# Half-block products after Strassen in 5 of 11 pairs of weight tiles of the down projections of a two-layer decoder

## The chip, the core and the metric

The kernel runs on one core of one Trainium2 chip. A core has five engines that run beside each other and meet through semaphores: TensorE (PE: matrix products, results into PSUM, 8 banks of 128 x 512 float32), VectorE (DVE) and ScalarE (ACT) (elementwise work), GpSimd (POOL), and SyncE (SP), whose queue starts the transfers from HBM to the on-chip memory (SBUF). The metric is device time in microseconds (us); less is better. The time before is the median of three runs.

## What is computed

Sequence 512, width 1024, inner width of the feed-forward part 2816, all float32, two layers. Layer 0 mixes tokens by pooling, layer 1 by attention; both end in the same feed-forward part, whose second product is what the change is about:

```python
def conv_ffn(h, w_up, conv_w, conv_b, w_down):
    u = h @ w_up
    u = causal_dwconv(u, conv_w, conv_b)
    a, g = jnp.split(u, 2, axis=-1)
    return (jax.nn.silu(g) * a) @ w_down

def reference(x, ...):
    for i in range(DEPTH):
        ...
        x = x + conv_ffn(rmsnorm(x, norm_g[i, 1]), w_up[i], conv_w[i], conv_b[i], w_down[i])
    return rmsnorm(x, final_norm)
```

So `w_down` is 2816 x 1024 per layer, and the left operand (the gated activation) is 512 x 2816.

## The kernel before

**Numbers.** Matrix products run in a reduced float32 format. To keep float32 accuracy every operand is split into a high and a low half (`split`, lines 141 to 144: ACT copies `hi`, DVE subtracts to get `lo`), and each product is three matmuls (`mm3`, lines 159 to 163): high x high, high x low, low x high.

**Tiles.** The 512 tokens are 4 tiles of 128 (index t), the 2816 inner channels 22 tiles of 128 (index f or k), taken in 11 pairs (kk). The 1024 output columns are two halves of 512 (dh). The residual stream stays in SBUF as `xt[t]`.

**Up projection** (`ffn`, lines 385 to 397). For each f two products give the gate and the value channel; `gate` (lines 376 to 383) does the convolution (`conv`), SiLU and the product, and splits the result into `ah`, `al`, tiles of 128 channels x 512 tokens from `big` (tag T, 44 buffers). These are the stationary operands of the down projection.

**Down projection** (lines 399 to 424). Per column half four PSUM banks, one per token tile, collect all 22 k tiles. `chunk` (lines 151 to 157) loads two k tiles of weights, 128 x 1024 float32, 512 KB, into `raw` (3 buffers) and takes `hi` and `lo` (5 buffers each); `split` fills these; then 2 k x 4 t x 3 matmuls of 128 x 128 by 128 x 512 follow. In the second half the last three chunks are kept and multiplied token tile by token tile, so that each bank is added into `xt` (line 423) while PE goes on with the next. `after(t, dh)` goes on from there: in layer 0 (`to_n2`) the norm and the transposes for the attention, in layer 1 (`finish`) the final norm and the output.

**Order.** Only PE's order is that of the program text (`manual_schedule` for PE around everything but the start). The instructions of DVE, ACT, POOL and the transfers are put in order by a planner at build time, by priority in the order of the text and by when it reckons that their inputs and buffers are there; so work that is ready can run well ahead of its place in the text. On the chip each engine takes its own queue in order. Buffers with one tag rotate: `wide` (tag h, 4 buffers of 128 x 1024) serves norms and scratch, `scratch` (tag w, 6 buffers of 128 x 512) the convolutions, `Normed` takes the two buffers of tag H (128 x 4096 each) for the transposed, split input of the up projection, `bank` the eight PSUM banks.

Of the kernel before, what the change touches and what calls it, by code (L numbers as in the profile page):

```python
# [8 lines left out]
F32 = mybir.dt.float32  # L9
F32R = mybir.dt.float32r  # L10
AF = mybir.ActivationFunctionType
ALU = mybir.AluOpType
AX = mybir.AxisListType

P = 128
S = 512
D = 1024
NT = S // P
KD = D // P
DFF = 2816  # L20
NF = DFF // P
H = 8
# [12 lines left out]
VALUES, WEIGH, TURN = 2, 3, 5  # L35
RATES = 1.34, .6, 1.0
START = 1
AT = [(2, 1), (3, 0)]
CONSTS = P + S + 2 * 4 * P + 4 * 16

# [23 lines left out]
def trunk(ctx, tc, x, norm_g, pool_w, pool_scale, kv_norm, w_kv, wq, lam, subln_g, wo,  # L64
          w_up, conv_w, conv_b, w_down, final_norm, consts, out):
    nc = tc.nc
# [3 lines left out]
    hp = ctx.enter_context(tc.tile_pool(name="hp", bufs=1))  # L70
# [7 lines left out]
    def bank(name):  # L78
        return psum.tile([P, S], F32, tag="ps", name=name)

    def big(name, dt=F32R):
        return tp.tile([P, S], dt, tag="T", bufs=44, name=name)
# [4 lines left out]
    def scratch(name, dt=F32):  # L87
        return work.tile([P, S], dt, tag="w", bufs=6, name=name)

    def wide(name):  # L90
        return work.tile([P, D], F32, tag="h", bufs=4, name=name)

    def v3(t, a):
        return t.rearrange("p (a b) -> p a b", a=a)
# [6 lines left out]
    xt = [const.tile([P, D], F32, name=f"x{t}") for t in range(NT)]  # L101
# [35 lines left out]
    for i in (1, 2):  # L137
        n = S if i == 1 else 64
        nc.sync.dma_start(out=bands[i][:, :n], in_=consts[:, P + S * (i + 1):P + S * (i + 1) + n])

    def split(src, hi, lo):

        nc.scalar.copy(hi, src)  # L143
        nc.vector.tensor_tensor(lo, src, hi, ALU.subtract)  # L144
# [6 lines left out]
    def chunk(src, a, b, name):  # L151

        raw = wp.tile([P, a * b], F32, tag="raw", bufs=3, name=f"raw_{name}")
        hi = wp.tile([P, a * b], F32R, tag="hi", bufs=5, name=f"hi_{name}")
        lo = wp.tile([P, a * b], F32R, tag="lo", bufs=5, name=f"lo_{name}")
        nc.sync.dma_start(out=v3(raw, a), in_=src)
        return raw, hi, lo

    def mm3(ps, l, r, first, last):
        (lh, ll), (rh, rl) = l, r  # L160
        nc.tensor.matmul(ps, lh, rh, start=first, stop=False)  # L161
        nc.tensor.matmul(ps, lh, rl, start=False, stop=False)  # L162
        nc.tensor.matmul(ps, ll, rh, start=False, stop=last)  # L163

    def cols(pair, a, b):
        return tuple(v[:, a:b] for v in pair)
# [73 lines left out]
    def up_chunk(l, m):  # L240
        return chunk(w_up[l, :, m * P:(m + 1) * P].rearrange("(k p) c -> p k c", p=P), KD, P, f"u{l}_{m}")

    def up_weights(l, m):
        raw, hi, lo = up_chunk(l, m)
        split(raw, hi, lo)
        return hi, lo
# [5 lines left out]
    def product(l, m, ps, w, hT, a, b):  # L252
        for k in range(KD):
            mm3(ps[:, a:b], cols(w, k * P, (k + 1) * P), hT.k(k, a, b), k == 0, k == KD - 1)
# [16 lines left out]
    r0, h0, pin, d, pw, pout, pup = {}, {}, {}, {}, {}, {}, {}  # L271
# [76 lines left out]
    def vectors(_):  # L348
# [6 lines left out]
                 s=pool_split, o=pool_out, r=pool_add, q=n1.rms, v=n1.scale, t=n1.turn, u=n1.split,  # L355
                 H=up_high, L=up_low, p=up_product, c=vectors, W=warm)
# [6 lines left out]
    def ffn(l, hT, cw, ws, pss, after):  # L363


        act = []

        def conv(ps, m, name):
            y = scratch(f"cv_{name}")
            w = [v[:, m:m + 1] for v in cw]  # L370
            nc.scalar.activation(y, ps, AF.Identity, bias=w[3], scale=w[2])
            nc.vector.scalar_tensor_tensor(y[:, 1:], ps[:, :S - 1], w[1], y[:, 1:], ALU.mult, ALU.add)
            nc.vector.scalar_tensor_tensor(y[:, 2:], ps[:, :S - 2], w[0], y[:, 2:], ALU.mult, ALU.add)
            return y

        def gate(f, pg, pa):
            y = conv(pg, NF + f, f"{l}_{NF + f}")
            nc.scalar.activation(y, y, AF.Silu)
            a = conv(pa, f, f"{l}_{f}")
            nc.vector.tensor_tensor(a, a, y, ALU.mult)  # L380
            ah, al = big(f"ah{l}_{f}"), big(f"al{l}_{f}")
            split(a, ah, al)
            act.append((ah, al))

        for n, w in enumerate(ws):
            product(l, n, pss[n], w, hT, S // 2, S)
        for f in range(EARLY):
            gate(f, pss[2 * f], pss[2 * f + 1])
        for f in range(EARLY, NF):
            pss = []  # L390
            for half in (1, 0):
                m = half * NF + f
                w = up_weights(l, m)
                ps = bank(f"pu{l}_{m}")
                product(l, m, ps, w, hT, 0, S)
                pss.append(ps)
            gate(f, *pss)

        held = 3
        for dh in range(2):  # L400
            pss = [bank(f"pd{l}{dh}{t}") for t in range(NT)]

            def down(t, kk, w):
                for k2 in range(2):
                    k = 2 * kk + k2
                    mm3(pss[t], cols(act[k], t * P, (t + 1) * P), cols(w, k2 * S, (k2 + 1) * S),
                        k == 0, k == NF - 1)

            kept = []
            for kk in range(NF // 2):  # L410
                raw, hi, lo = chunk(w_down[l, kk * 2 * P:(kk + 1) * 2 * P, dh * S:(dh + 1) * S]
                                    .rearrange("(k p) c -> p k c", p=P), 2, S, f"d{l}_{dh}_{kk}")
                split(raw, hi, lo)
                if dh == 1 and kk >= NF // 2 - held:
                    kept.append((kk, (hi, lo)))
                    continue
                for t in range(NT):
                    down(t, kk, (hi, lo))
            for t in range(NT):
                for kk, w in kept:  # L420
                    down(t, kk, w)
                part = xt[t][:, dh * S:(dh + 1) * S]
                nc.vector.tensor_tensor(part, pss[t], part, ALU.add)
                after(t, dh)

    n2 = Normed("n2", None)

    def to_n2(t, dh):
# [3 lines left out]
        if t > 1:  # L432
            n2.tensors(t - 2)

    ffn(0, n1, cw0, [w[1:] for w in up0], pup, to_n2)


# [5 lines left out]
                      in_=lam.rearrange("l a b -> l (a b)").to_broadcast([P, 4 * HD]))  # L443
# [149 lines left out]
    def wo_add(ps, t, dh):  # L593
        part = xt[t][:, dh * S:(dh + 1) * S]
        nc.vector.tensor_tensor(part, ps, part, ALU.add)
# [67 lines left out]

    for i in range(START):
        next(filler)
# [19 lines left out]
    for t in range(2, NT):  # L685
        for dh in range(2):
            ps = bank(f"pw4{t}{dh}")
            for h in range(4, H):
                wo_part(ps, t, dh, h, h == 4, h == H - 1)
            wo_add(ps, t, dh)  # L690
            if (t, dh) in AT:
                n3.tensors(AT.index((t, dh)))
        n3.vectors(t)
# [27 lines left out]
    for n in range(2 * EARLY):  # L721
        raw, hi, lo = up_chunk(1, (n + 1) % 2 * NF + n // 2)
        split(raw, hi, lo)
        up1.append((hi, lo))
    for n in range(2 * EARLY):
        pup.append(bank(f"pu1_{n}"))
        product(1, n, pup[n], up1[n], n3, 0, S // 2)
        if n in (0, 1):
            n3.tensors(2 + n)
    ffn(1, n3, [columns(r) for r in conv_rows(1)], up1, pup, finish)  # L730


# [29 lines left out]
```

## Time and profile before

| | |
|---|---|
| median of 3 runs | 1008.89 us (1007.28 to 1009.53) |
| the profiled execution's own time | 1007.95 us |
| its span, first to last instruction | 1006.2 us |
| up projection of layer 0, most of it (65.0 to 279.6) | 214.6 us |
| down projection of layer 0 (279.6 to about 403) | about 123 us, the next norm's transposes among it |
| down projection of layer 1 (about 880 to 999) | about 119 us |
| HBM read / written | 92.44 MB / 2.10 MB |

The rest of the span is the pooling (to about 40 us) and the attention (about 403 to 650 us). How to read the lines that follow below: a row of the groups gives line, engine, operation, output and inputs, shapes and count, then total busy time and the mean of one in ns, then the idle time of that engine just before and what ended it. A row of the timeline begins with start and duration in us, and ends with the idle time before it and its releaser. A row of the stretches gives its bounds, its length, and each engine's busy time with the number of instructions, then PE's granted clock, the share of the DMA engines and GB/s. PE is the matmul, PEld the loading of the stationary operand beside it. A line number can be a helper's: line 144 is every low half, line 143 every high half, lines 161 to 163 every matmul of `mm3`; the name of the tile tells which (`pd` the down banks, `pu` the up banks, `d` in `raw_d`, `hi_d`, `lo_d` the down weights).

### The profile page before, as it was taken

Reading aid. Unit: us, or ns where it says so; the run is one execution under the profiler, and the core shown is the slowest. Engines: PE = TensorE matmul, PEld = TensorE weight load, DVE = VectorE, ACT = ScalarE, POOL = GpSimd, SP = SyncE. Lnnn points to the kernel's source line nnn. Section 1 sums busy time; section 2 is a strip of 40 time slices with the busy share of each in tenths; the row PEclk is TensorE's granted clock in tenths of the full one; section 3 lists DMA queues with packets and bytes.
Section 4 is the critical chain, followed back from the end, with each engine's and each line's share of the span. In section 5 each row is a group of like instructions: output and inputs, shape, how many; then the busy total and the mean of one; then the engine's idle time right before and its main releaser. Section 6 shows DMA issues by size and latency. Waiting matters only on the chain.

```text
span 1006.2 us, 12339 instructions
## 1 busy us (share of the span) xinstructions
PE 991.4 (99%) x4870; PEld 838.3 (83%) x4870; DVE 569.7 (57%) x872; ACT 426.9 (42%) x671; POOL 85.7 (9%) x113
## 2 busy tenths in 40 slices
PE   8999999999999999999999999999999999999997
PEld 8998888888888888778888887988888888888885
DVE  5766656656632323557766797576566566532213
ACT  5554443444432213446756662464444434422211
POOL 4500000000000001261220101000000000000001
PEclk9999999999999999999999999999999999999999
DMA  7333233233232321243213111243332332332312
GB/s 259 109 105 105 85 104 101 88 105 94 94 110 85 114 98 49 71 139 105 64 42 105 64 43 42 84 126 95 94 105 88 101 104 85 105 94 95 105 42 83
DMA packets 128707, 95.33 MB, mean 95 GB/s; under 512 B 3329, under 2 KB 111498, under 8 KB 128650
## 3 DMA queue, kind: packets, MB, share of 16 engines
q1 hardware_dynamic: 128650, 94.55, 30.4%
q8 instruction: 38, 0.62, 0.2%
q14 instruction: 19, 0.16, 0.0%
HBM read 92.44 MB, written 2.10 MB: 94 GB/s over the span
## 4 chain that ended last, share of the span: by engine, by line
PE 96%; DVE 1%; DMA 1%; ACT 0%; issue 0%; SPq 0%; POOL 0%; DVEq 0%; POOLq 0%; ACTq 0%
PE pu L161 16%; PE pu L162 16%; PE pu L163 16%; PE pd L163 8%; PE pd L161 8%; PE pd L162 8%; PE sc L531 2%; PE po L560 2%; PE pw L163 1%; PE pj_k L161 1%; PE pj_k L162 1%; PE pw L162 1%; PE pw L161 1%; PE pj_k L163 1%; PE pj_q L162 1%; PE pj_q L161 1%
## 5 line engine op out<-in xcount | busy, mean ns | idle before, releaser
L144 DVE TENSOR_TENSOR lo_u<-raw_u,hi_u 128x1024 fp32r<-128x1024 f32 x84 | 103.3, 1232 | 126.9 <-ACT hi_u L143 126.7
L161 PE MATMUL pu<-n3h,hi_u 128*128 128x512 f32 (+1 forms) x384 | 142.9, 372 | 0.0
L161 PE MATMUL pu<-n1h,hi_u 128*128 128x512 f32 (+1 forms) x384 | 142.8, 372 | 0.0
L162 PE MATMUL pu<-n3l,hi_u 128*128 128x512 f32 (+1 forms) x384 | 142.6, 371 | 0.0
L162 PE MATMUL pu<-n1l,hi_u 128*128 128x512 f32 (+1 forms) x384 | 142.6, 371 | 0.0
L163 PE MATMUL pu<-n1h,lo_u 128*128 128x512 f32 (+1 forms) x384 | 142.6, 371 | 0.0
L163 PE MATMUL pu<-n3h,lo_u 128*128 128x512 f32 (+1 forms) x384 | 142.6, 371 | 0.0
L144 DVE TENSOR_TENSOR lo_d<-raw_d,hi_d 128x1024 fp32r<-128x1024 f32 x44 | 53.9, 1226 | 147.1 <-ACT hi_d L143 147.1
L161 PE MATMUL pd<-hi_d,ah 128*128 128x512 f32 x352 | 137.0, 389 | 0.0
L163 PE MATMUL pd<-hi_d,al 128*128 128x512 f32 x352 | 136.9, 389 | 0.0
L162 PE MATMUL pd<-lo_d,ah 128*128 128x512 f32 x352 | 136.9, 389 | 0.0
L143 ACT CAST hi_u<-raw_u 128x1024 fp32r<-128x1024 f32 x84 | 88.1, 1051 | 64.2 <-PE pu L162 59.4
L143 ACT CAST hi_d<-raw_d 128x1024 fp32r<-128x1024 f32 x44 | 46.2, 1050 | 142.0 <-PE pd L163 131.3
L161 PEld LDWEIGHTS pu<-n1h,hi_u 128*128 128x128 f32 x384 | 72.3, 188 | 12.6
L163 PEld LDWEIGHTS pu<-n3h,lo_u 128*128 128x128 f32 x384 | 72.3, 188 | 12.6
L163 PEld LDWEIGHTS pu<-n1h,lo_u 128*128 128x128 f32 x384 | 72.3, 188 | 12.5
L162 PEld LDWEIGHTS pu<-n3l,hi_u 128*128 128x128 f32 x384 | 72.4, 188 | 12.5
L161 PEld LDWEIGHTS pu<-n3h,hi_u 128*128 128x128 f32 x384 | 72.3, 188 | 12.4
L162 PEld LDWEIGHTS pu<-n1l,hi_u 128*128 128x128 f32 x384 | 72.4, 188 | 12.3
L162 PEld LDWEIGHTS pd<-lo_d,ah 128*128 128x128 f32 x352 | 66.1, 188 | 13.7
L163 PEld LDWEIGHTS pd<-hi_d,al 128*128 128x128 f32 x352 | 66.1, 188 | 13.7
L161 PEld LDWEIGHTS pd<-hi_d,ah 128*128 128x128 f32 x352 | 66.1, 188 | 13.6
(146 smaller groups left out, 1553.2 us busy)
## 6 DMA issues: line engine op xcount, KB each, us to landing
raw_u<-in_w_up_dram SPq DMA_DIRECT2D x88, 512.0 KB, 3.7
raw_d<-in_w_down_dram SPq DMA_DIRECT2D x44, 512.0 KB, 3.3
raw_v<-in_w_kv_dram SPq DMA_DIRECT2D x8, 512.0 KB, 3.6
raw_q<-in_wq_dram SPq DMA_DIRECT2D x8, 512.0 KB, 4.0
raw_k<-in_w_kv_dram SPq DMA_DIRECT2D x8, 512.0 KB
raw_o<-in_wo_dram SPq DMA_DIRECT2D x8, 512.0 KB, 4.9
x<-in_x_dram SPq DMA_DIRECT2D x4, 512.0 KB
out_dram<-y SPq DMA_DIRECT2D x8, 256.0 KB, 2.1
```

The costliest lines, as they stand in the source:

```text
L143: nc.scalar.copy(hi, src)
L144: nc.vector.tensor_tensor(lo, src, hi, ALU.subtract)
L161: nc.tensor.matmul(ps, lh, rh, start=first, stop=False)
L162: nc.tensor.matmul(ps, lh, rl, start=False, stop=False)
L163: nc.tensor.matmul(ps, ll, rh, start=False, stop=last)
L531: nc.tensor.matmul(ps[:, :m], qs[h, c][:, q], k[:, :m], start=not last, stop=bool(last))
L560: nc.tensor.matmul(po[h][:, qi * P:(qi + 1) * P], aT[:, kt * P:(kt + 1) * P], vt[kt][h // 4][:, (h % 4) * VD:(h % 4 + 1) * VD], start=kt = ...
```

## The change

In pairs kk 0 to 4 (SEVEN = 5) of both layers' down projections, the product of two k tiles is made as Strassen's scheme for a 2 x 2 block matrix. The blocks of the left operand are: token half (left 256, right 256) by k tile of the pair; those of the weights: k tile of the pair by column half. Seven products of a 256-token block by a 128 x 512 block stand in place of eight.

- `forms` makes, for one pair, the token-side blocks on DVE: a sum over 512 columns, three over 256, then splits into high and low (256 and 3 x 512 columns). Pairs 0 and 1 get theirs at the end of their `gate`, in the up projection. Pairs 2 to 4 (LATE = 2) leave `gate` unsplit, as a float32 tile each, and get theirs in the down projection (steps f2, f3, f4), in rooms made of the two H buffers, which the up projection has given up by then, and in T buffers.
- `product_weights` loads for product i one or two weight blocks per pair (`SIDES`; the second into a `wide` tile), adds or subtracts the second on DVE, and splits. The five pairs are taken in groups a (pairs 0, 1), b (2, 3), c (4): 512, 512 and 256 KB per block.
- `seven` multiplies: per pair two token tiles x 3 matmuls, into two banks of the product's own. Product 7 adds into the two left banks of the first half, product 6 into the two right banks of the second half, since each goes into one place only.
- `put_all` (step e with the product's number) adds or subtracts a product's two banks into `xt` at its places (`PLACES`). Step s adds the right banks of the first half, step d calls `after(t, 0)`.
- `PASSES` gives PE's order for the two halves: p0 to p5 are pairs 5 to 10 done plainly (24 matmuls), 5a is product 5 of group a (12 matmuls; group c 6), k3 to k5 the kept pairs. The `n2` and `finish` steps and the last loop over t stay.

```diff
--- before
+++ after
@@ -35,6 +35,20 @@
 VALUES, WEIGH, TURN = 2, 3, 5
 RATES = 1.34, .6, 1.0
 START = 1
+HALF = S // 2
+SEVEN, LATE = 5, 2
+GROUPS = (0, 2), (2, 2), (4, 1)
+
+
+SIDES = {1: ((0, 0), ALU.add, (1, 1)), 2: ((0, 0), None, None), 3: ((0, 1), ALU.subtract, (1, 1)),
+         4: ((1, 0), ALU.subtract, (0, 0)), 5: ((1, 1), None, None), 6: ((0, 0), ALU.add, (0, 1)),
+         7: ((1, 0), ALU.add, (1, 1))}
+PLACES = {1: ((0, 0, ALU.add), (1, 1, ALU.add)), 2: ((1, 0, ALU.add), (1, 1, ALU.subtract)),
+          3: ((0, 1, ALU.add), (1, 1, ALU.add)), 4: ((0, 0, ALU.add), (1, 0, ALU.add)),
+          5: ((0, 0, ALU.subtract), (0, 1, ALU.add)), 7: ((0, 0, ALU.add),)}
+
+PASSES = ("p0 5a p1 f2 2a 7a f3 p2 f4 5b 5c e5 p3 2b 2c e2 p4 1a 1b p5 s 1c e1 7b 7c e7",
+          "p0 4a 4b p1 4c e4 d 3a p2 3b 3c e3 6a 6b 6c k3 k4 k5")
 AT = [(2, 1), (3, 0)]
 CONSTS = P + S + 2 * 4 * P + 4 * 16
 
@@ -363,10 +377,11 @@
     def ffn(l, hT, cw, ws, pss, after):
 
 
-        act = []
-
-        def conv(ps, m, name):
-            y = scratch(f"cv_{name}")
+        act, form = {}, {}
+
+        def conv(ps, m, name, y=None):
+            if y is None:
+                y = scratch(f"cv_{name}")
             w = [v[:, m:m + 1] for v in cw]
             nc.scalar.activation(y, ps, AF.Identity, bias=w[3], scale=w[2])
             nc.vector.scalar_tensor_tensor(y[:, 1:], ps[:, :S - 1], w[1], y[:, 1:], ALU.mult, ALU.add)
@@ -374,13 +389,41 @@
             return y
 
         def gate(f, pg, pa):
+            late = LATE <= f // 2 < SEVEN
             y = conv(pg, NF + f, f"{l}_{NF + f}")
             nc.scalar.activation(y, y, AF.Silu)
-            a = conv(pa, f, f"{l}_{f}")
+            a = conv(pa, f, f"{l}_{f}", big(f"ar{l}_{f}", F32) if late else None)
             nc.vector.tensor_tensor(a, a, y, ALU.mult)
-            ah, al = big(f"ah{l}_{f}"), big(f"al{l}_{f}")
-            split(a, ah, al)
-            act.append((ah, al))
+            if f // 2 < SEVEN:
+                act[f] = a
+                if f % 2 and not late:
+                    forms(f // 2, big)
+            else:
+                ah, al = big(f"ah{l}_{f}"), big(f"al{l}_{f}")
+                split(a, ah, al)
+                act[f] = ah, al
+
+        left, right = slice(0, HALF), slice(HALF, S)
+
+        def forms(kk, room):
+
+
+            a, b = act.pop(2 * kk), act.pop(2 * kk + 1)
+            f = wide(f"f{l}_{kk}")
+            add, less = ALU.add, ALU.subtract
+            nc.vector.tensor_tensor(v3(f[:, :S], 2), v3(a, 2), b[:, right].unsqueeze(1).to_broadcast([P, 2, HALF]), add)
+            nc.vector.tensor_tensor(f[:, S:S + HALF], a[:, left], b[:, left], add)
+            nc.vector.tensor_tensor(f[:, S + HALF:], a[:, right], a[:, left], less)
+            nc.vector.tensor_tensor(b[:, left], b[:, left], b[:, right], less)
+            name = f"{l}_{kk}"
+            both = room(f"fa{name}")
+            split(a[:, left], both[:, left], both[:, right])
+            form[kk, 3] = both[:, left], both[:, right]
+            for src, one, two in (f[:, :S], 1, 2), (f[:, S:], 5, 6), (b, 7, 4):
+                hi, lo = room(f"fh{name}_{one}"), room(f"fl{name}_{one}")
+                split(src, hi, lo)
+                form[kk, one] = cols((hi, lo), 0, HALF)
+                form[kk, two] = cols((hi, lo), HALF, S)
 
         for n, w in enumerate(ws):
             product(l, n, pss[n], w, hT, S // 2, S)
@@ -396,32 +439,95 @@
                 pss.append(ps)
             gate(f, *pss)
 
-        held = 3
+
+        halls = [hp.tile([P, KD * S], F32R, tag="H", bufs=2, name=f"hall{l}{i}") for i in range(2)]
+        rooms = [v[:, i * S:(i + 1) * S] for v in halls for i in range(KD)]
+
+        def room(name):
+            return rooms.pop() if rooms else big(name)
+
+        def weights(kk, n, j, dh, name, tag=None):
+
+            src = w_down[l, kk * 2 * P:(kk + n) * 2 * P, dh * S:(dh + 1) * S]
+            src = src.rearrange("(k j p) c -> p j k c", j=2, p=P)[:, j]
+            if tag:
+                raw = wide(f"raw2_{name}")[:, :n * S]
+                nc.sync.dma_start(out=v3(raw, n), in_=src)
+                return raw
+            return chunk(src, n, S, name)
+
+        def product_weights(i, kk, n):
+            name = f"d{l}_{i}_{kk}"
+            (j, dh), op, other = SIDES[i]
+            raw, hi, lo = weights(kk, n, j, dh, name)
+            if op:
+                more = weights(kk, n, *other, name, True)
+                nc.vector.tensor_tensor(raw, raw, more, op)
+            split(raw, hi, lo)
+            return hi, lo
+
+        def seven(i, kk, n, pss, first=None, last=None):
+
+            w = product_weights(i, kk, n)
+            for t in range(2):
+                for k in range(n):
+                    mm3(pss[t], cols(form[kk + k, i], t * P, (t + 1) * P), cols(w, k * S, (k + 1) * S),
+                        kk + k == first, kk + k == last)
+
+        def pair_weights(kk, dh):
+            raw, hi, lo = chunk(w_down[l, kk * 2 * P:(kk + 1) * 2 * P, dh * S:(dh + 1) * S]
+                                .rearrange("(k p) c -> p k c", p=P), 2, S, f"d{l}_{dh}_{kk}")
+            split(raw, hi, lo)
+            return hi, lo
+
+        def pair(ps, t, kk, w, first=False, last=False):
+            for k in range(2):
+                mm3(ps, cols(act[2 * kk + k], t * P, (t + 1) * P), cols(w, k * S, (k + 1) * S),
+                    first and k == 0, last and k == 1)
+
+        def put(ps, t, dh, op=ALU.add):
+            part = xt[t][:, dh * S:(dh + 1) * S]
+            nc.vector.tensor_tensor(part, part, ps, op)
+
+        def put_all(i):
+            for half, dh, op in PLACES[i]:
+                for t in range(2):
+                    put(at[i][t], 2 * half + t, dh, op)
+
+        at, kept = {}, []
         for dh in range(2):
             pss = [bank(f"pd{l}{dh}{t}") for t in range(NT)]
-
-            def down(t, kk, w):
-                for k2 in range(2):
-                    k = 2 * kk + k2
-                    mm3(pss[t], cols(act[k], t * P, (t + 1) * P), cols(w, k2 * S, (k2 + 1) * S),
-                        k == 0, k == NF - 1)
-
-            kept = []
-            for kk in range(NF // 2):
-                raw, hi, lo = chunk(w_down[l, kk * 2 * P:(kk + 1) * 2 * P, dh * S:(dh + 1) * S]
-                                    .rearrange("(k p) c -> p k c", p=P), 2, S, f"d{l}_{dh}_{kk}")
-                split(raw, hi, lo)
-                if dh == 1 and kk >= NF // 2 - held:
-                    kept.append((kk, (hi, lo)))
-                    continue
-                for t in range(NT):
-                    down(t, kk, (hi, lo))
-            for t in range(NT):
-                for kk, w in kept:
-                    down(t, kk, w)
-                part = xt[t][:, dh * S:(dh + 1) * S]
-                nc.vector.tensor_tensor(part, pss[t], part, ALU.add)
-                after(t, dh)
+            at[7 - dh] = pss[2 * dh:2 * dh + 2]
+            for step in PASSES[dh].split():
+                if step[0] == "f":
+                    forms(int(step[1:]), room)
+                elif step[0] == "p":
+                    kk = SEVEN + int(step[1:])
+                    w = pair_weights(kk, dh)
+                    for t in range(NT):
+                        pair(pss[t], t, kk, w, kk == SEVEN, dh == 0 and kk == NF // 2 - 1 and t > 1)
+                elif step[0] == "k":
+                    kk = SEVEN + int(step[1:])
+                    kept.append((kk, pair_weights(kk, dh)))
+                elif step[0] == "e":
+                    put_all(int(step[1:]))
+                elif step[0] == "s":
+                    for t in (2, 3):
+                        put(pss[t], t, 0)
+                elif step[0] == "d":
+                    for t in range(NT):
+                        after(t, 0)
+                else:
+                    i, (kk, n) = int(step[0]), GROUPS["abc".index(step[1])]
+                    if i not in at:
+                        at[i] = [bank(f"pd{l}_{i}{t}") for t in range(2)]
+                    own = i < 6
+                    seven(i, kk, n, at[i], 0 if own else None, SEVEN - 1 if own or i == 7 else None)
+        for t in range(NT):
+            for kk, w in kept:
+                pair(pss[t], t, kk, w, last=kk == NF // 2 - 1)
+            put(pss[t], t, 1)
+            after(t, 1)
 
     n2 = Normed("n2", None)
 
```

## The prediction

> **What bounds the kernel now.** I read the head of the page first, then the waits of TensorE (PE), then the order of time inside a down projection.
>
> ```profile
> span 1006.2 us, 12339 instructions
> PE 991.4 (99%) x4870; PEld 838.3 (83%) x4870; DVE 569.7 (57%) x872; ACT 426.9 (42%) x671; POOL 85.7 (9%) x113
> PEclk9999999999999999999999999999999999999999
> PE 96%; DVE 1%; DMA 1%; ACT 0%; issue 0%; SPq 0%; POOL 0%; DVEq 0%; POOLq 0%; ACTq 0%
> ```
>
> PE is busy for 99% of the span, at the full granted clock in all 40 slices, and the chain that ended last runs through it for 96%. The ends of matmuls are modelled, so "busy" could still hide waits; hence the waits of PE, longest first:
>
> ```profile
> engine line waited for: us in total, times, longest us
> PE pv L163 <- DVE n2l L144: 1.9, 1, 1.9
> PE sc L531 <- DVE kl L514: 1.6, 1, 1.6
> PE dps L309 <- DVE h L199: 1.3, 1, 1.3
> ```
>
> None is in a down projection (tile pd). There only the number of matmuls times their spacing counts. The spacing shows on VectorE (DVE), which follows PE in this stage: it makes the low half of one weight chunk each time PE has released a buffer.
>
> ```profile
> 297.40 1.22 DVE L144 TENSOR_TENSOR lo_d<-raw_d,hi_d 128x1024 fp32r<-128x1024 f32 x1 [4.21 <-ACT hi_d L143]
> ...
> 335.48 1.23 DVE L144 TENSOR_TENSOR lo_d<-raw_d,hi_d 128x1024 fp32r<-128x1024 f32 x1 [4.21 <-ACT hi_d L143]
> ```
>
> Between these two starts lie seven steps of one chunk, each 24 matmuls (2 k tiles x 4 token tiles x 3 products of high and low): 38.08 / 168 = **0.2267 us** per matmul. The Trainium skill (TensorE: Matmul & The Clock Gate, "Back-to-back issue gap") gives N / 2.4 + 2.5 ns, which is 215.8 ns for 512 columns; the trace's 226.7 is longer, and the measurement decides.
>
> **The matmuls.** One pair of k tiles costs 24 matmuls per column half before, 48 in all. Of the seven products each takes 2 token tiles x 3 = 6 per pair, together 42. Five pairs in two layers save 5 x 2 x 6 = 60 matmuls of the same shape, 60 x 0.2267 = **13.60 us**; a down stage goes from 528 to 498 matmuls, from 119.7 to 112.9 us. By the page's gap it would be 60 x 0.2158 = 12.9 us, an estimate. PE's order is written by hand before and after, so only waits can take this back, and the count rules out that the change doesn't do what it says.
>
> **What is added, and what covers it.** All of it lies on DVE, ScalarE (ACT) and the DMA queue; the cover is PE's 112.9 us per stage.
>
> ```profile
> L144 DVE TENSOR_TENSOR lo_d<-raw_d,hi_d 128x1024 fp32r<-128x1024 f32 x44 | 53.9, 1226 | 147.1 <-ACT hi_d L143 147.1
> L143 ACT CAST hi_d<-raw_d 128x1024 fp32r<-128x1024 f32 x44 | 46.2, 1050 | 142.0 <-PE pd L163 131.3 <-PE pu L162 7.0 <-issue 3.8
> L144 DVE TENSOR_TENSOR al<-cv,ah 128x512 fp32r<-128x512 f32 x44 | 30.5, 692 | 27.0 <-ACT ah L143 27.0
> L143 ACT CAST ah<-cv 128x512 fp32r<-128x512 f32 x44 | 27.3, 621 | 111.5 <-DVE cv L380 111.5
> L423 DVE TENSOR_TENSOR x<-pd,x 128x512 f32<-128x512 f32 x16 | 10.8, 688 | 17.5 <-PE pd L163 17.0
> L149 DVE SCALAR_TENSOR_TENSOR pwl<-pw,c_gn,pwh 128x256 fp32r<-128x256 f32 x4 | 2.1, 594 | 0.0
> ```
>
> DVE in one layer's down stage:
> - Low halves of weights: 12 plain chunks and 14 double groups (7 products, groups a and b) at 1.226 are 31.9; 7 single groups (c) at 0.692 are 4.8.
> - Sums of two weight blocks (products 1, 3, 4, 6, 7), same shapes: 10 x 1.226 + 5 x 0.692 = 15.7.
> - The forms of a pair: a sum over 512 columns and three over 256, then low halves of 256 and three of 512. No row has a sum of two tensors over 256 columns. It lies between half of the 512-column row, 0.346, and the 256-column row above, 0.594; I take 0.425, on the line through the 512 and 1024 rows. The repeated operand of the first sum is taken at the plain 0.692. That is 0.692 + 3 x 0.425 + 0.425 + 3 x 0.692 = 4.47 (4.15 to 5.15 by the two ends). Three pairs fall into this stage: 13.4.
> - Additions into x: 11 places x 2 token tiles, 2 in step s, 4 last: 28 x 0.688 = 19.3 (8 before).
>
> Sum 85.1. What else DVE does in the stage stays:
>
> ```profile
> core 0: us, PE busy (x) PEld busy (x) DVE busy (x) ACT busy (x) POOL busy (x), PEclk, DMA share, GB/s
> 65.00:279.60 214.60, 214.60 (x949) 177.75 (x948) 132.38 (x160) 92.92 (x119) 0.00 (x0) 1.00 0.33 100
> 279.60:336.60 57.00, 57.00 (x253) 47.23 (x252) 17.01 (x21) 14.22 (x15) 0.00 (x0) 1.00 0.29 94
> 336.60:399.00 62.40, 62.40 (x281) 51.76 (x280) 18.35 (x24) 13.76 (x17) 3.48 (x5) 1.00 0.27 89
> ...
> 575.00:625.00 50.00, 49.17 (x278) 41.91 (x277) 41.35 (x104) 25.51 (x61) 4.77 (x9) 1.00 0.15 45
> ```
>
> Of 17.01 + 18.35 in the down stage 18 low halves and 7 additions are 26.9, so 8.5 are other work; and the first four chunks are split ahead of the stage (22 low halves in all), 4.9 us. So 85.1 + 8.5 - 4.9 = **89 us of 112.9, 79%**. The last row is a stage of the attention as dense as that: DVE 83%, and PE lost 0.83 us in 50. In the up projection (first row) DVE is at 62%; there the two early pairs add 4.47 - 2 x 0.692 = 3.1 us each and the three late ones take 1.4 each away, +2.0 us against 82 free. ACT comes to some 38 us of 112.9.
>
> Transfers:
>
> ```profile
> raw_d<-in_w_down_dram SPq DMA_DIRECT2D x44, 512.0 KB, 3.3
> mask<-consts_dram SPq DMA_DIRECT2D x1, 256.0 KB, 2.7
> ```
>
> Before, 22 loads of 512 KB per stage; after, 36 of 512 and 12 of 256: 22 MB in 112.9 us, 195 GB/s. By the window of the first half 94 GB/s are a share of 0.29, so full use is some 324 GB/s, and this is 60% of it. The densest stretch, 4a to 6c of the second half, loads 8.9 MB in 31.3 us of PE: 285 GB/s, 88%. It fits, with four chunks of lead in the five buffers.
>
> **Where something can be late**, DVE's work added up against PE's from the stage's first matmul:
>
> ```profile
> 283.44 0.22 DVE L447 TENSOR_TENSOR lamt<-lamt 128x64 f32<-128x64 f32 x1
> 284.94 0.69 DVE L144 TENSOR_TENSOR al<-cv,ah 128x512 fp32r<-128x512 f32 x1 [0.17 <-ACT ah L143]
> ...
> 338.48 0.69 DVE L423 TENSOR_TENSOR x<-pd,x 128x512 f32<-128x512 f32 x1 [0.57 <-PE pd L163]
> 339.84 0.69 DVE L423 TENSOR_TENSOR x<-pd,x 128x512 f32<-128x512 f32 x1 [0.67 <-PE pd L163]
> 340.92 1.23 DVE L144 TENSOR_TENSOR lo_d<-raw_d,hi_d 128x1024 fp32r<-128x1024 f32 x1 [0.39 <-ACT hi_d L143]
> ```
>
> ```profile
> L161 PE MATMUL pd<-hi_d,ah x352: 389/389/477, 279.8 to 998.2; 128*128 128x512 f32 x176
> ```
>
> - The opening. PE began the stage at 279.8, and DVE ended the last gate at 285.6, 5.8 us later. PE reaches 5b after 108 matmuls, 24.5 us. By then DVE owes 5.8, 7a 2.45, p2 1.23, the forms of pairs 2, 3, 4 13.4 and 5b 1.23: 24.1, all but level. Two things relieve it: only 5c, 2.7 us later, wants pair 4; and the sums of late pairs have had their inputs since the up stage, where the planner can run them, as it ran L447 far ahead of its place in the program: 3 x 1.97 = 5.9 us less.
> - The added waits. Twenty more additions wait for PE, and low halves stand behind them in DVE's queue. Before, two additions waited 0.57 and 0.67, and the low half behind them still started at 340.92, 5.44 after 335.48, on the beat. The lead of four chunks hides that; a shorter one would show each wait.
> - The densest stretch. A chunk can be split once PE has released the one five places back. Added up so, the closest is k4, ready near 94.7 and wanted at 97.9.
> - PSUM banks. Eight at most are held. The closest are those that step s frees near 55.8, wanted by p0 of the second half at 59.8.
> - The ends (three kept pairs, one token tile at a time, 18 matmuls each) stay.
>
> I charge 0.5 us of new waits per layer, 1.0 in all, between 0 and the attention row's loss (0.83 in 50, so 3.7 in 226). The profiled execution took 1007.95 us around its span, 0.9 under the median of 1008.89: 1007.95 - 13.60 + 1.0 = 995.35, or 996.3 against the median. I say **996**.
>
> **Rivals.**
> 1. *The opening is late.* Say nothing is run ahead and the splits of the late forms hold DVE for half of ACT's copies (3 x 0.621 + 0.35 per pair, 6.6 for three, half is 3.3): 5b comes 24.1 + 3.3 - 24.5 = 2.9 us late, 5.8 over two layers: 1000. With all of it 6.2 and 12.4: 1007. For: 24.1 against 24.5. Against: L447. Chance 0.20.
> 2. *DVE bounds the whole stage: slower.* DVE takes its queue in order. If it stands still for ACT's copy ahead of every low half, it needs 89 + 22 x 1.05 + 7 x 0.62 + 6.6 = 123.0 us, 10.1 over PE, 20.2 over two layers: 1007.95 - 13.6 + 20.2 = 1014.6. Of these 34 us the first 24 cost nothing, and the sign turns at 31. For: all idle time ahead of lo_d is put down to hi_d (147.1). Against: hi_d itself had waited 131.3 for PE, so that idle time was to spare; and the attention row. The Trainium skill (TensorE: Matmul & The Clock Gate, "Architectural detail") says that ACT and DVE are strictly first in, first out; the trace agrees, with 340.92 behind 339.84. Chance 0.10.
> 3. *Loads come round too slowly.* A summed chunk holds one of three raw buffers for landing, sum, copy and low half, 3.3 + 1.23 + 1.05 + 1.23 = 6.8 us: one per 2.3 us, PE's takes 2.72. If the traffic, or a second buffer held by the forms, doubles the landing, it is one per 3.4: the 11 chunks of the densest stretch take 37.1 against 31.3, 5.8 late per layer with the lead spent, 1.3 with half of it. In the middle, 3.5: 1001. Chance 0.10.
>
> **How the numbers follow.** Forecast (993.5 to 998.5) 0.60, rivals 0.20, 0.10, 0.10. The low end is the lowest time before, 1007.28, less 13.6. The high end, 1005, leaves out rival 2, 0.05 of rival 1, 0.03 of rival 3, and 0.02 lie under the low end. A measurement of this kernel can tell about 0.2%, 2 us, from no change. Faster: 0.60 + 0.16 + 0.08 of rivals 1 and 3. Same: 0.03, 0.02 and 0.01 of rivals 1, 3 and 2. Slower: 0.09 of rival 2 and 0.01 of rival 1.
>
> **What would show it.** Right: 4810 matmuls, no wait of PE over 1 us in the down stages, DVE near 80% there, a span near 994. Rival 1: PE waits for DVE's forms at the first group of product 5 that takes late pairs. Rival 2: PE waits for low halves all through, DVE over 95%. Rival 3: DVE's weight sums wait for DMA. The forecast is wrong if the spacing is no longer 0.2267 without any wait, or if the waits exceed 2 us per layer.

## The result and the profile after

| | before | after |
|---|---|---|
| median | 1008.09 us (4 runs) | 991.79 us (4 runs) |
| the profiled execution's own time | 1007.95 | 991.28 |
| its span | 1006.2 | 989.5 |

The ratio is 0.9845, 95% interval 0.9817 to 0.9873. The gain was forecast in sign, but it is larger than forecast: the median lies 1.7 us under the low end of the range and 4.2 us under the forecast.

First the head of the page and the waits of TensorE (PE) of the kernel after:

```profile
span 989.5 us, 12580 instructions
PE 978.0 (99%) x4810; PEld 826.9 (84%) x4810; DVE 664.8 (67%) x1024; ACT 451.1 (46%) x713; POOL 86.9 (9%) x113
PE 94%; DVE 2%; DMA 1%; POOL 1%; ACT 1%; issue 0%; SPq 0%; POOLq 0%; DVEq 0%; ACTq 0%
...
raw_d<-in_w_down_dram SPq DMA_DIRECT2D x72, 512.0 KB, 3.4
raw_d<-in_w_down_dram SPq DMA_DIRECT2D x24, 256.0 KB, 3.0
```

```profile
engine line waited for: us in total, times, longest us
PE dps L323 <- DVE h L213: 1.2, 1, 1.2
PE warm L144 <- DVE ones L139: 1.0, 1, 1.0
PE pw L175 <- ACT oh L162: 0.8, 1, 0.8
PE pv L177 <- DVE n2l L158: 0.7, 1, 0.7
PE pp L176 <- DVE pwl L158: 0.5, 2, 0.4
PE pp L176 <- DVE pwl L163: 0.2, 1, 0.2
```

PE has 60 matmuls less and no wait in a down projection. But two waits elsewhere are not what they were: pv on n2l had 1.9, now 0.7; sc on kl had 1.6 and is gone. Both sit at the entry of the attention, right behind layer 0's down projection. To see where the 16.7 us of span went, four marks are read from the starts of PE's tiles (first and last start, per tile). Of before and of after, the rows that give the marks between the stages:

```profile
L531 PE MATMUL sc<-kh,qs x64: 278/363/481, 451.5 to 599.8; 128*128 128x256 f32 x32, 128*128 128x384 f32 x16, 128*128 128x512 f32 x16
...
L161 PE MATMUL pu<-n3h,hi_u x384: 277/389/396, 636.2 to 878.5; 128*128 128x512 f32 x160, 128*128 128x256 f32 x32
```

```profile
L637 PE MATMUL sc<-kh,qs x64: 277/363/481, 443.5 to 590.1; 128*128 128x256 f32 x32, 128*128 128x384 f32 x16, 128*128 128x512 f32 x16
...
L175 PE MATMUL pu<-n3h,hi_u x384: 278/389/396, 626.6 to 868.9; 128*128 128x512 f32 x160, 128*128 128x256 f32 x32
```

Stretch A runs from the first pd to the first score (sc), B from there to layer 1's first pu, C from its last pu to its last pd (layer 1's down projection alone). All runs of this study, in us:

| kernel | A | B | C | span |
|---|---|---|---|---|
| before | 171.7 | 184.7 | 119.6 | 1006.2 |
| after | 163.7 | 183.1 | 112.9 | 989.5 |
| layer1_only | 173.2 | 184.5 | 112.9 | 1002.1 |
| layer0_only | 164.0 | 183.1 | 119.7 | 997.7 |
| before_q00_dve | 170.3 | 184.8 | 119.7 | 1004.9 |
| before_h01_dve | 169.6 | 184.7 | 119.6 | 1004.2 |
| before_q21_pieces | 171.6 | 183.3 | 119.7 | 1005.7 |
| before_both | 169.6 | 183.0 | 119.6 | 1003.2 |
| dose1 | 164.8 | 183.0 | 112.9 | 991.9 |
| dose2 | 171.3 | 183.1 | 120.4 | 1006.2 |
| after_again | 163.8 | 183.1 | 112.9 | 990.2 |
| after_both | 164.6 | 183.1 | 112.9 | 990.6 |

A moves a little with the clock as well: in layer1_only, where layer 0 is as before, it is 1.5 us longer than before, with a granted clock of 0.50 from some 412.1 to 415.5 (0.71 over 410 to 415, where before has 1.00).

C is the change by itself, as it was reckoned: 119.6 to 112.9, 6.7 us for 30 matmuls. A gained 8.0, which is 6.8 and 1.2 more; B, in which nothing was changed, gained 1.6. With 0.1 in layer 1's up projection and 0.3 behind the last matmul that is 16.7. The 1.2 and 1.6 us beyond the matmuls are the two waits: 1.9 - 0.7 in A and 1.6 - 0 in B, 2.8 together.

### The profile page after: what moved, and what is told of

The parts are those of the page before. It is cut to its first block, busy times and chain, and to the rows that moved or that the text cites. A ratio compares the mean times of both kernels' runs of the same rounds, so it can differ in the third digit from the quotient of the medians.

```text
span 989.5 us, 12580 instructions
## 1 busy us (share of the span) xinstructions
PE 978.0 (99%) x4810; PEld 826.9 (84%) x4810; DVE 664.8 (67%) x1024; ACT 451.1 (46%) x713; POOL 86.9 (9%) x113
## 4 chain that ended last, share of the span: by engine, by line
PE 94%; DVE 2%; DMA 1%; POOL 1%; ACT 1%; issue 0%; SPq 0%; POOLq 0%; DVEq 0%; ACTq 0%
PE pu L175 16%; PE pu L176 16%; PE pu L177 16%; PE pd L175 7%; PE pd L177 7%; PE pd L176 7%; PE sc L637 2%; PE po L666 2%; PE pw L177 2%; PE pj_k L175 1%; PE pj_k L177 1%; PE pj_q L175 1%; PE pj_k L176 1%; PE pj_q L176 1%; PE pj_q L177 1%; PE pw L176 1%
## 5 line engine op out<-in xcount | busy, mean ns | idle before, releaser
L157 ACT CAST hi_d<-raw_d 128x1024 fp32r<-128x1024 f32 (+1 forms) x66 | 63.6, 963 | 119.5 <-PE pd L177 86.4
L158 DVE TENSOR_TENSOR lo_d<-raw_d,hi_d 128x1024 fp32r<-128x1024 f32 (+1 forms) x66 | 72.3, 1109 | 29.5 <-ACT hi_d L157 29.4
L175 PE MATMUL pd<-hi_d,ah 128*128 128x512 f32 x192 | 74.8, 389 | 0.0
L177 PE MATMUL pd<-hi_d,al 128*128 128x512 f32 x192 | 74.7, 389 | 0.0
L176 PE MATMUL pd<-lo_d,ah 128*128 128x512 f32 x192 | 74.7, 389 | 0.0
L394 ACT ACTIVATE cv<-cv 128x512 f32<-128x512 f32 x44 | 27.9, 634 | 81.1 <-DVE cv L388 81.0
L386 ACT ACTIVATE cv<-pu,c_cb,c_cw 128x512 f32<-128x512 f32 x76 | 58.8, 773 | 0.0
L388 DVE SCALAR_TENSOR_TENSOR cv<-pu,c_cw,cv 128x510 f32<-128x510 f32 x76 | 56.9, 748 | 2.4
```

## The experiments

**Theory A:** each layer gains its 30 matmuls times the spacing, and the rest are two waits at the entry of the attention that came out otherwise, for reasons outside the arithmetic of the change. **Theory B:** a removed matmul is worth more than the spacing, 16.7 / 60, wherever it is removed.

**One layer at a time.** The kernel after with the old function kept beside the new one, and called for one layer (arguments shortened):

```diff
-    ffn(0, n1, cw0, ...)
+    plain_ffn(0, n1, cw0, ...)      # layer1_only
-    ffn(1, n3, ...)
+    plain_ffn(1, n3, ...)           # layer0_only
```

> Layer 0's down projection is as before, layer 1's has the seven products. Theory A (each layer gains 30 matmuls x 0.2267 = 6.8 us, and the 3 us beyond 13.6 are two waits of TensorE at the entry of the attention that came out otherwise): 6.8 to 7.1 us faster than before, near 1001.1, and the waits pv on n2l (1.9) and sc on kl (1.6) are both still there. Theory B (a removed matmul is worth more than the spacing, 16.7 / 60 = 0.278 us, in either layer): 8.3 us faster, near 999.8.

> Layer 1's down projection is as before, layer 0's has the seven products. Theory A: 6.8 us for the matmuls and up to 2.8 more where the two waits at the entry of the attention shrink as in the changed kernel (pv on n2l 0.7, sc on kl gone): near 998.5. Theory B: 8.3 us, near 999.8, and the layer's share shows in the stage itself, not in these waits.

Measured: layer1_only 999.32 us, 0.9921 of before (0.9894 to 0.9948), layer0_only 1000.55 us, 0.9922 (0.9895 to 0.9949). The medians alone lie nearer to theory B's 999.8 than to A's 1001.1 and 998.5, but these intervals, 5 us wide, can't tell 6.8 from 8.3; the stretches can. Layer 1's stage gains 6.7 (C in layer1_only), and layer 0's 6.8 (A in layer0_only is 7.7 shorter, 0.9 of it the wait pv on n2l). With layer 0 plain the two waits stay, as the list of PE's waits of layer1_only shows:

```profile
PE pv L177 <- DVE n2l L158: 1.8, 1, 1.8
PE sc L700 <- DVE kl L683: 1.4, 1, 1.4
```

With layer 0 changed and layer 1 plain, only pv on n2l is left, with 1.0. So a removed matmul is worth its spacing, and the extra belongs to layer 0's change and to these waits: theory B falls.

**Why pv waited.** GpSimd (POOL) and VectorE (DVE) of the kernel before, at the end of layer 0's down projection, in the timeline (start and duration in us, instruction, in brackets what it waited for and how long):

```profile
389.96 1.90 POOL L483 TENSOR_TENSOR raw_q<-raw_q,c_gn 128x1024 f32<-128x1024 f32 x1 [346.49 <-DMA raw_q<-in_wq_dram]
391.94 0.22 POOL L181 TENSOR_SCALAR r_n<-ssq_n 128x1 f32<-128x1 f32 x1
```

```profile
392.85 0.88 DVE L199 TENSOR_SCALAR sq_n<-x,r_n 128x512 f32<-128x512 f32 x2 [4.72 <-POOL r_n L184]
393.65 0.68 DVE L423 TENSOR_TENSOR x<-pd,x 128x512 f32<-128x512 f32 x1
```

ScalarE (ACT) had the sum of squares of token tile 0 ready at 389.3, as its timeline shows:

```profile
389.13 0.18 ACT L191 ACTIVATION_READ_ACCUMULATOR sq_n<-x 128x1 f32 x1
```

POOL's queue had the gain of the first query weights (q00) ahead of the norm's r_n, so r_n began 2.6 us late; DVE's queue had the scaling by r_n ahead of the addition of tile 1, and so the lateness went on to tiles 1, 2 and 3. In the kernel after, q00's loading starts 0.1 us behind tile 0's addition, not 1.9 ahead of it, and the planner put r_n first:

```profile
383.27 0.22 POOL L195 TENSOR_SCALAR r_n<-ssq_n 128x1 f32<-128x1 f32 x1 [339.79 <-ACT sq_n L205]
383.58 0.57 POOL L198 TENSOR_TENSOR r_n<-r_n,halfneg 128x1 f32<-128x1 f32 x1
385.69 1.90 POOL L589 TENSOR_TENSOR raw_q<-raw_q,c_gn 128x1024 f32<-128x1024 f32 x1 [1.54 <-DVE x L490]
```

The test takes that instruction out of POOL's queue in the kernel *before*:

```diff
-        nc.gpsimd.tensor_tensor(v3(raw, KD), v3(raw, KD), spread(g, P), ALU.mult)
+        eng = nc.vector if name == "q00" else nc.gpsimd
+        eng.tensor_tensor(v3(raw, KD), v3(raw, KD), spread(g, P), ALU.mult)
```

> The kernel before, with the gain of the first query weight chunk (q00) multiplied on VectorE instead of GpSimd; nothing else. Theory A (that one instruction of 1.90 us stood ahead of the norm of token tile 0 in GpSimd's queue and made the four norms late): GpSimd's first r_n of the second norm starts within 0.5 us after ScalarE's sum of squares (2.6 before), the additions into x for tiles 1 to 3 come up to 2 us earlier, and pv on n2l shrinks from 1.9 to 0.7 or less: 1.2 us faster, near 1006.9. If something else makes the norms late: wait 1.9, time 1008.1.

POOL's first r_n in this run:

```profile
389.53 1.31 POOL L181 TENSOR_SCALAR r_n<-ssq_n 128x1 f32<-128x1 f32 x1 [345.93 <-ACT sq_n L191]
```

Measured: r_n starts 0.1 us after the sum of squares, at 389.53; the wait falls from 1.9 to 0.4; A is 1.4 shorter; 0.998 of before (0.9967 to 0.9992). As theory A had it.

**Why sc waited.** The low half of q20 on DVE and the gain of q21 on POOL, in the kernel before, then the same two in the kernel after:

```profile
449.78 1.90 POOL L483 TENSOR_TENSOR raw_q<-raw_q,c_gn 128x1024 f32<-128x1024 f32 x1 [1.77 <-DMA raw_q<-in_wq_dram]
```

```profile
449.88 2.87 DVE L144 TENSOR_TENSOR lo_q<-raw_q,hi_q 128x1024 fp32r<-128x1024 f32 x1 [2.16 <-ACT hi_q L143]
```

```profile
441.91 1.23 DVE L158 TENSOR_TENSOR lo_q<-raw_q,hi_q 128x1024 fp32r<-128x1024 f32 x1 [1.84 <-ACT hi_q L157]
```

```profile
442.19 2.71 POOL L589 TENSOR_TENSOR raw_q<-raw_q,c_gn 128x1024 f32<-128x1024 f32 x1 [1.83 <-DMA raw_q<-in_wq_dram]
```

Where POOL starts 0.10 us first, DVE's 1.23 us become 2.87; where DVE starts 0.28 first, POOL's 1.90 become 2.71 and DVE loses nothing. kl stands behind that low half in DVE's queue, and PE waits for kl. The same pair meets in nine of the runs (in the other three q21's gain is cut in pieces). POOL is first in before, layer1_only, before_q00_dve and before_h01_dve, by 0.04 to 0.35 us, and PE waits 1.4 to 1.7 for kl; DVE is first in after, layer0_only, dose1, dose2 and after_again, by 0.15 to 0.81, and the wait is gone. In all nine the head start and the time of the one that comes second add up to 2.97 to 2.99 us.

What turned the order is small. In before and in after the low half starts 1.11 us after PE begins its pj_q matmuls (448.77 and 440.80). POOL's gain starts 1.01 after that in before and 1.39 in after: its load goes out when the low half of the key chunk ahead is done, which in after comes 0.3 later against PE. Why it does was not followed further back. So 0.38 us of order was worth 1.6 us, and that this change turned it was luck.

My first test of this named the wrong chunk:

```diff
-        nc.gpsimd.tensor_tensor(v3(raw, KD), v3(raw, KD), spread(g, P), ALU.mult)
+        eng = nc.vector if name[1] in "01" else nc.gpsimd
+        eng.tensor_tensor(v3(raw, KD), v3(raw, KD), spread(g, P), ALU.mult)
```

> The kernel before, with the gains of the query and key weights of the first two head pairs (8 chunks) multiplied on VectorE instead of GpSimd. Theory A (the wait sc on kl came from a low half of 1.23 us that took 2.87 beside a GpSimd instruction of 1.90): no low half over 1.4 us before the first scores, the wait on kl gone, and pv on n2l at 0.7 or less: up to 2.8 us faster, near 1005.3. If VectorE's own load (8 x 1.23 more) is what counts there: waits of TensorE for lo_q, lo_k or kl of 1 us and more, no gain.

Measured: 0.999 of before (0.9976 to 1.0005); pv's wait is gone, A 2.1 shorter, but sc waits 1.7 for kl as before, and B stays at 184.7. POOL still had an instruction of 1.90 us beside the low half, which took 2.92:

```profile
447.79 1.90 POOL L484 TENSOR_TENSOR raw_q<-raw_q,c_gn 128x1024 f32<-128x1024 f32 x1 [1.50 <-DMA raw_q<-in_wq_dram]
```

```profile
447.85 2.92 DVE L144 TENSOR_TENSOR lo_q<-raw_q,hi_q 128x1024 fp32r<-128x1024 f32 x1 [2.16 <-ACT hi_q L143]
```

Counted off in POOL's queue the colliding instruction is the gain of q21, of the third head pair, which this edit leaves on POOL. So the second test (before_q21_pieces) cuts just that one into four:

```diff
-        nc.gpsimd.tensor_tensor(v3(raw, KD), v3(raw, KD), spread(g, P), ALU.mult)
+        step = 2 if name == "q21" else KD
+        for i in range(0, KD, step):
+            part = v3(raw, KD)[:, i:i + step]
+            nc.gpsimd.tensor_tensor(part, part, spread(g[:, i:i + step], P), ALU.mult)
```

> The kernel before, with the gain of query chunk q21 multiplied on GpSimd in four pieces of 256 columns instead of one instruction of 1.90 us. Theory A (VectorE and GpSimd exclude each other for a whole instruction, the one that starts first holds, and this one started 0.10 us ahead of the low half of q20): the low half there takes at most 1.9 us instead of 2.87, and the wait of TensorE sc on kl falls from 1.6 to 0.7 or less; about 1 us faster in the span between the two marks. If lo_q was slow for another reason: 2.87 and 1.6 stay.

The same low half of q20 in the timeline of DVE of before_q21_pieces (start, duration):

```profile
450.91 1.41 DVE L144 TENSOR_TENSOR lo_q<-raw_q,hi_q 128x1024 fp32r<-128x1024 f32 x1 [2.15 <-ACT hi_q L143]
```

The low half takes 1.41, the wait on kl is 0.2, B is 183.3. The whole time can't show 1.4 us here: 0.9999 of before (0.9982 to 1.0015). Then both edits in the kernel before:

> The kernel before with both edits: q00's gain on VectorE and q21's gain on GpSimd in four pieces. Theory A: both waits at the entry of the attention (pv on n2l, sc on kl) fall to 0.7 or less each, so that first scores start 2 to 2.8 us earlier than in the kernel before, with no half-block product in it; this accounts for nearly all of the 3.1 us that the change gave beyond 13.6. If they need the change: the sum of the two waits stays over 2.

Measured: neither wait is in the list; A and B are 2.1 and 1.7 shorter; 0.9971 of before (0.996 to 0.9982), 2.9 us. So what the change gave beyond its matmuls is to be had without it. (Here DVE's low half started at 448.54, 0.25 us ahead of POOL's first piece, and took 1.23: the order had turned already, so this run doesn't show what the pieces are worth; before_q21_pieces does.)

**Both edits in the kernel after,** beside the kernel after on the same chip:

> The changed kernel once more, beside the next one on the same chip. Theory A and its rival alike: near 991.8, TensorE's waits at the entry of the attention together under 1 us.

> The changed kernel with the two edits of the kernel before_both (q00's gain on VectorE, q21's gain on GpSimd in four pieces). Theory A (the change had already removed most of the two waits by moving when things start): only the remaining 0.7 us of pv on n2l can go, 0 to 1 us faster than after_again, near 991.2. If the two edits help in another way than by these waits, they give the 2.9 us here too: near 988.9.

Measured: 992.65 and 993.36 us. The gain of the change repeats, and so do its waits: A is 163.8 and 164.6, B is 183.1 in both, so there was nothing left of the second wait; pv waits 0.8 and 1.5. In after_both q00's gain stands in DVE's queue (385.54, 1.23 us) ahead of the addition of tile 1 (386.68), which in the kernel after follows tile 0's scaling at once. The edits don't help here, and the ratios to before, 0.9856 (0.9838 to 0.9874) and 0.9864 (0.9847 to 0.9881), don't tell the two kernels apart. No version here beats the kernel after.

**How much cover was left.** The kernel after with one or two unused sums of DVE behind each sum of two weight blocks:

```diff
                 nc.vector.tensor_tensor(raw, raw, more, op)
+                nc.vector.tensor_tensor(more, raw, more, op)      # once or twice
```

> The changed kernel with one more VectorE sum behind every sum of two weight blocks (its result is not used): 10 x 1.226 + 5 x 0.692 = 15.7 us more VectorE work per down stage, 89 + 15.7 = 105 of 112.9 us, 93%. If the load alone decides: no TensorE wait over 1 us in the down stages, time within 2 us of the changed kernel's 991.8. If hand-offs between ScalarE and VectorE are exposed, as rival 2 had it: 4 us and more slower.

> The changed kernel with two more VectorE sums behind every sum of two weight blocks (results not used): 89 + 31.4 = 120.4 us of VectorE work per down stage against 112.9 of TensorE. If the load alone decides: 7.5 us late per stage, 15 us slower in all, near 1007. If hand-offs count too: 20 us and more. If VectorE has more room than the sum says (work run ahead into the stages beside it): under 10.

Measured: dose1 993.57 us, 0.9864 of before (0.9834 to 0.9894), C 112.9: 13.5 us more of DVE work per stage cost nothing there. (A is 1.1 longer, and pv's wait 1.7 again.) dose2 1008.14 us, 1.0007 (0.999 to 1.0024): the gain is gone, with 7.5 us more per stage. PE waits in both stages:

```profile
PE pd L175 <- ACT hi_d L157: 6.1, 2, 3.1
PE pd L176 <- DVE lo_d L158: 2.2, 2, 1.2
```

My sum for the stage gave just 7.5, and for the wrong reason. These are stretches of layer 1's down projection in dose2 (start and end, length, PE, PEld, DVE, ACT, POOL busy, PE's granted clock, DMA share, GB/s):

```profile
878.20:998.80 120.60, 116.47 (x500) 95.19 (x498) 100.19 (x120) 38.43 (x57) 2.60 (x6) 0.97 0.48 158
878.00:900.00 22.00, 22.00 (x99) 18.22 (x98) 15.67 (x22) 12.77 (x21) 0.00 (x0) 1.00 0.49 165
...
955.00:960.00 5.00, 5.00 (x23) 4.14 (x23) 5.00 (x7) 3.05 (x8) 0.00 (x0) 1.00 0.76 254
960.00:965.00 5.00, 5.00 (x23) 4.13 (x22) 5.00 (x7) 1.60 (x4) 0.00 (x0) 1.00 0.34 96
965.00:970.00 5.00, 5.00 (x23) 3.92 (x22) 5.00 (x7) 0.54 (x1) 0.00 (x0) 1.00 0.43 150
970.00:975.00 5.00, 1.85 (x7) 0.88 (x5) 5.00 (x7) 1.56 (x2) 0.00 (x0) 0.96 0.30 105
975.00:980.00 5.00, 4.01 (x10) 3.18 (x11) 5.00 (x6) 1.05 (x1) 0.00 (x0) 0.50 0.33 105
980.00:985.00 5.00, 5.00 (x21) 4.07 (x20) 2.39 (x3) 2.09 (x2) 0.00 (x0) 0.86 0.66 210
```

DVE isn't full over the stage (100.19 of 120.60 us, 83%, first row; 71% in its first 22 us), but it is full in the densest stretch, until PE's lead is spent; then PE waits 3.1 us and, soon after, 1.0. The starts of PE's matmuls show where the 7.5 us go. Two gaps, from 970.85 to 974.32 and on to 975.99, last 3.47 and 1.67 in place of 0.227: 4.7 us. The 13 steps behind them take 5.57 us in place of 2.95, most of them 0.43 apart: 2.6 us more, at a granted clock of 0.50. Layer 0's stage does the same (waits of 3.1 and 1.2, clock 0.50 from some 377 to 384).

## Why the prediction was wrong, point by point

- *The matmuls, 13.60:* right. Stretch C fell by 6.7 and layer 0's part of A by 6.8, 13.5 together; the count is 4810.
- *The cover:* right in what it concluded, and DVE's load was oversized. The counts of added instructions are those of the trace, and the sum over 256 columns, taken at 0.425, took 0.418 to 0.426. But DVE was busy for 65% of layer 1's stage, not 79%, by the stretch of the kernel after that holds it (columns as above):

```profile
869.30:982.30 113.00, 113.00 (x500) 93.47 (x498) 73.86 (x92) 38.90 (x57) 2.59 (x6) 1.00 0.51 168
```

  The sums of the late forms, 5.9 us, all ran ahead in the up stage, and neighbours overlap: four additions took 2.48, 0.62 each, where the row that the prediction took has a mean of 0.688, as in this row of the timeline of DVE in the kernel after:

```profile
307.86 2.48 DVE L490 TENSOR_TENSOR x<-x,pd 128x512 f32<-128x512 f32 x4 [1.10 <-PE pd L177]
```

- *The opening (rival 1):* did not happen. The last low half of the late forms ended at 293.1, 13.3 us into layer 0's stage, where I had reckoned 22.9 (24.1 less 5b's own low half, 1.23); 5b began on the beat, at 304.3, 24.5 us in.
- *Rivals 2 and 3:* did not happen. Rival 3's sign was seen, for DVE waited for the loads of weight sums (8.1 us in layer 0's stage, longest 3.6; 9.9 in layer 1's, longest 4.5), but PE waited for nothing in either stage, so it cost nothing. That a doubled dose brings the gain to nothing shows that rival 2's side was there; but it acts in the densest stretch, not over the whole stage as rival 2 had it.
- *The charge of 1.0 for new waits:* wrong, 0 in the down stages.
- *The step that failed:* I listed PE's waits, saw that "None is in a down projection", and put their change at nothing in the sum 1007.95 - 13.60 + 1.0. Two of those very rows, 1.9 and 1.6, hang on when the stage ahead ends and on what stands in front of what in the queues; the change moved that, and 2.8 of their 3.5 us went (1.2 of the first, all of the second). I had bounds for new waits from 0 upwards and none for old waits that go: the low end should have been lower by the 3.5. I had given 0.02 to a time under it.
- *The base:* I added 0.9 for the median over the profiled execution; after the change it is 0.5. So 996.3 less 1.0 (the charge), 2.8 (the waits), 0.4 (that offset) and 0.4 (outside the stretches) is about 991.7, against 991.8 measured.

It is shown that the two waits went, and that each goes without the change if its cause is taken away. Why the planner, given the changed stage, put r_n first was not tried; it was only seen in the order. Nor was it shown what shifted the gain of q21 by the 0.38 us that turned the second pair.

## What to carry to other kernels

Where one engine sets the time, the count of its instructions times their spacing, taken from a chain in the trace, gives what a removed instruction is worth to 0.1 us in 6.7. But each wait in that engine's list is a term of the sum too: behind a stage that gets shorter or busier ask of each what it hangs on, and let the range go below the count by the waits that may vanish. And cover is to be reckoned in the densest stretch against the lead of the buffers, not as a share of the stage.

## What the runs showed of the hardware

- DVE and POOL exclude each other, nearly for a whole instruction, where DVE subtracts two operands in SBUF beside POOL's gain: 0.10 us of head start decided whether DVE's 1.23 us became 2.87 or POOL's 1.90 became 2.71. Over nine runs the head start and the second one's time add up to 2.97 to 2.99 us, against 3.13 for the two one after the other. Even the 0.22 us r_n took 1.31 beside the gain on DVE. The Trainium skill (SBUF — State Buffer, "SBUF: two separate sides") says that the pair of ports shared by the two is an exclusive lock, held by whoever starts first for the whole instruction, where the DVE instruction has two inputs in SBUF and POOL's reads SBUF; these runs agree. It isn't so for every pair: in before, DVE's qs, with one input in PSUM, started at 445.70 amid a gain of 1.95 us on POOL (from 445.48) and took 0.69 us, its usual time.
- A wait of 3.1 us on PE cost clock too: right after it ended the granted clock fell to 0.50 for some 7 us, in both stages of dose2, so that 4.7 us of gaps brought 2.6 more. The Trainium skill (TensorE: Matmul & The Clock Gate, "HAM oscillation — how this bites in real kernels") has PE throttled to half after a gap of some 3.4 us; the 0.50 agrees, after a wait a little shorter. A shorter wait was followed by it too, 1.8 us in layer1_only (0.50 for some 3.4 us), while 1.9 us in before was not.
